# Eight stores of values in the second half: issued from ScalarE's queue in place of GpSimd's

## The chip, the cores and the metric

The kernel runs on one core of one Trainium2 chip. The metric is the device time of one execution in microseconds. The core has five instruction queues: TensorE (PE, with its weight loads PEld), VectorE (DVE), ScalarE (ACT), GpSimd (POOL) and SyncE (SP). DMAs are issued from the queues of SP, ACT and GpSimd and all run on the core's 16 DMA engines.

## The reference

One layer of a streaming encoder over two groups with the same weights: a prompt of 2048 tokens and a sample of 32, model width 1024. Cut to what matters:

```python
h = rmsnorm(x, g_pre_mix)
z = h @ w_in                                   # 1024 -> 512 + 4 * 512
u, zq, zf, zi, zg = split(z)                   # zi: the values of the recurrence
y_pool = pool_mix(u, ...)                      # trailing-window means, per-group map
q, f, k = silu(zq), lb + (1 - lb) * sigmoid(zf), (1 - lb) * sigmoid(-zf)
S1, o = hgrn_run(S0, q, k, zi, log(f))         # 4 heads x 128, state 128 x 128 per head
y_hg = rmsnorm(o, g_hg_norm) * silu(zg)
x = x + rmsnorm(concat(y_pool, y_hg) @ w_out, g_post_mix)
f = (silu(h2 @ w_gate) * (h2 @ w_up)) @ w_down # h2 = rmsnorm(x, g_pre_ffn), 1024 -> 2816 -> 1024
x = x + rmsnorm(f, g_post_ffn)
```

Everything is in float32.

## The kernel before

The prompt is worked through in two halves of 1024 tokens, the sample beside the second. Each half has the stages values and projections with recurrence (`front`), output projection (`project`), and `gate_up`; `down` comes once behind both. A float32 product is made of three matmuls of a high and a low part (`fhi`, `flo` for activations, `wf` for weights). In the second half the projections are made by a seven-product scheme: `front_pairs` runs over eight pairs of column blocks, each with seven products of twelve 128x512 matmuls, and accumulates them in PSUM banks that the code calls `gx`, `gz`, `gy`. For the first pair (f and q of head 0) the products stand in the order gx, gz, gx, gy, gx, gy, gx. The weight forms of each product lie in DRAM (`wd`) and are loaded as two tiles `wf` three products ahead (`fetch`, L929).

Ahead of them `values` multiplies the 1024 tokens by the 512 value columns. It fills all eight PSUM banks (`vps`), four of the pool MM and four of AX. In its last round it copies each bank to a tile `vt` of 128 x 4 x 128, four on ScalarE and four on VectorE in turn (L809), and stores each in DRAM (`vd`, four heads of 128 x 8 x 128, in pieces of 512 bytes) from GpSimd's queue (L810). Later `hgrn` loads the values of one head as `vh` (L1192). The same PSUM banks are then taken by gx, gz and gy.

What follows on the other engines for the first pair, with the lines that the prediction names:

- ScalarE copies the first gx to c (L956); PE then goes on in the same bank with the third product. VectorE adds gz to c (L959). ScalarE makes two sigmoids sg of c (`use`, L864 and L868), the first with a load of its function table ahead of it, then copies gx to another c (L967) and gy to a third (L971); the fifth product adds to the bank that L967 reads.
- In between, ScalarE and VectorE finish the high and low parts `hhi` and `hlo` of the first half's hidden values (L1525, L1528), SP stores them (`hdFalse`, L1530), and SP loads `xwv` (L817), weights for the sample's values (`vsps`).

`vt`, `c`, `sg`, `wf`, `xwv`, `hhi`, `hlo` and some others share the buffers of one pool, `tp`, with one tag and 25 buffers of 128 x 512 float32. A tile gets a buffer that an earlier tile has done with, and its first writer waits until the last reader of that one has ended; for vt the last reader is its store.

PE's order is the order of the program: small tasks are mixed in between products at points that a count of PE's planned time (`Pace.t`, `poll`) gives. The order of the other queues is chosen by the framework when the program is built, from the program's order and a plan of its own.

Of the kernel before, what the change touches and what calls it, by code (L numbers as in the profile page):

```python
# [84 lines left out]
def body(tc, ins, outs, cst):  # L85
    nc = tc.nc
    ctx = ExitStack()
    with ctx:
# [15 lines left out]
        def mmbank(name="mmb"):  # L104
            return MM.tile([P, 512], F32, tag="mm", name=name)

        def axbank(name="axb"):
            return AX.tile([P, 512], F32, tag="ax", name=name)
# [4 lines left out]
        def t2(name, shape=None, dt=F32):  # L113
            return TP.tile(shape or [P, 512], dt, tag="t", name=name)
# [90 lines left out]
        def mm(out, l, r, start, stop, ns, more=False):  # L205
            nc.tensor.matmul(out, l, r, start=start, stop=stop, skip_group_check=more)  # L206
            Pace.t += ns

        def rcost(n):
            return max(107.0, n / 2.4 + 2.5)  # L210
# [19 lines left out]
        def poll():  # L230
            for tk in list(Pace.tasks):
                if tk.done or (tk.after is not None and not tk.after.done):
                    continue
                if tk.ready <= Pace.t:
                    tk.step()
# [57 lines left out]
        def take(look=LOOK):  # L293
            i = Stream.used
            Stream.used += 1
            ahead(i + 1 + look)
            r = Stream.items[i]
            Stream.items[i] = None
            return r

        def in_turn(trios):

            for a, b in ((0, 2), (0, 3), (1, 2)) if len(trios) > 1 else ((0, 2), (1, 2), (0, 3)):
                for t in trios:
                    yield t[a], t[b]
# [134 lines left out]
        vd = DP.tile([NH, P, NCH, P], F32, name="vd")  # L440
# [351 lines left out]
        def values(S, pairs):  # L792
            pss = [mmbank("vps") for _ in range(4)] + [axbank("vps") for _ in range(4)]
            for k in range(0, KD, 2):
                _, hi, lo = take(1)
                while S.seen[0] < k + 2:
                    S.norm.step()
                if k == 4:
                    next(pairs)
                for i in range(8):  # L800
                    c0 = i % 4 * P
                    trios = [(*(x[:, kk * 512 + c0:kk * 512 + c0 + P] for x in S.plain[i // 4][k // 2]), hi[kk], lo[kk]) for kk in range(2)]
                    for n, (a, b) in enumerate(in_turn(trios)):
                        mm(pss[i], a, b, k == 0 and n == 0, k + 2 == KD and n == 5, rcost(512))
                        if n % 3 == 2:
                            poll()
                    if k + 2 == KD:
                        vt = t2("vt", [P, NH, P])
                        (nc.vector.tensor_copy if i % 2 else nc.scalar.copy)(vt, pss[i].rearrange("p (h c) -> p h c", c=P))  # L809
                        nc.gpsimd.dma_start(out=vd[:, :, i, :].rearrange("h p c -> p h c"), in_=vt)  # L810
            Smp.mix = Task(sample_mix(), 4000.0)

        def sample_values():
# [1232 lines left out]
        with tc.manual_schedule(engines={mybir.EngineType.PE}):  # L2046
            for i, S in enumerate(halves):
                if i:
                    while S.seen[0] < 1:
                        S.norm.step()  # L2050
                    pairs = front_pairs(S)
                    values(S, pairs)
                if i == 0:
                    halves[1].st = CP.tile([P, 64], F32, name="st_b")
                    Task(later_stats(halves[1]), 25000.0)
                    Task(mixed_weights(), 4000.0)
                if i:
                    next(pairs, None)
                else:
                    for h in range(NH):  # L2060
                        head_products(S, h)
                    for g in (3, 2, 1, 0):
                        pool_products(S, g)
                S.gpm = row_vector("g_post_mix")
                for tg in range(2):
                    project(S, tg)
                if i == 0:
                    forms = Task(weight_forms(), 50000.0)
                gate_up(S, second_start if i == 0 else (lambda: down_first(halves)))
            last = down(halves)  # L2070
            for tk in list(Pace.tasks):
                tk.finish()
# [42 lines left out]
```

## Time and profile before

| | |
|---|---|
| median of three runs | 2081.92 us (2081.21 to 2084.04) |
| profiled execution, its time | 2080.79 us |
| profiled execution, its span | 2079.0 us |
| mean granted clock of TensorE | 0.995 |
| DMA over the span | 389.15 MB, 187 GB/s |
| the stage of the change | 840 to 911 us of the span |

A time in the profile is in microseconds from the start of the span. A row of a timeline has start, busy time, engine, line, operation, output<-input, shape, and in brackets how long the engine sat idle before it and what released it. A row of the waits says who waited for whom: total, times, longest. "issue" is time in which an engine waited for nothing that the profile shows. A queue's DMA issue is listed by the time that the queue spent on it; "landing" is from the issue to the arrival of the last byte.

### The profile page before, as it was taken

The numbers are of one execution on the slowest core, as the hardware profiler recorded it, in microseconds if no ns is written. First come the engines' busy times: TensorE is split into PE (matmuls) and PEld (weight loads), VectorE is DVE, ScalarE is ACT, GpSimd is POOL, SyncE is SP. The second block draws the span as 40 slices with busy tenths as digits, with TensorE's granted clock in tenths as the row PEclk, the third lists the DMA queues.
The fourth block names the chain that finished last, engine by engine and source line by source line (L and its number), as shares of the span: only waits on it lengthen the run. The fifth ranks groups of instructions, "written<-read, shape, count | busy, mean of one in ns | idle before, by whom it ended". The sixth has DMA issues, their size and how long they took to land.

```text
span 2079.0 us, 34579 instructions
## 1 busy us (share of the span) xinstructions
PE 2050.9 (99%) x12980; PEld 1669.0 (80%) x12980; DVE 1464.9 (70%) x2252; ACT 850.8 (41%) x1689; POOL 413.9 (20%) x484
## 2 busy tenths in 40 slices
PE   9999999999999999799999999999999999999998
PEld 8788888888888887678887788888888778888876
DVE  5555674799887888666676697776666766566587
ACT  6544344654554544333344563444444521011032
POOL 0223421212222221333242100000000210110134
PEclk9999999999999999899999999999999999999999
DMA  8633344537787778464573614554445797776779
GB/s 290 200 101 113 103 142 143 171 109 236 226 245 216 219 217 253 152 239 151 194 267 132 193 51 137 163 149 145 138 142 167 235 336 221 220 224 200 220 199 225
DMA packets 427672, 389.15 MB, mean 187 GB/s; under 512 B 22360, under 2 KB 324432, under 8 KB 427504
## 3 DMA queue, kind: packets, MB, share of 16 engines
q1 hardware_dynamic: 424288, 376.65, 57.7%
q0 software_dynamic: 2784, 9.70, 2.2%
q8 instruction: 103, 1.69, 0.3%
q14 instruction: 65, 0.53, 0.1%
q10 hardware_dynamic: 432, 0.57, 0.1%
HBM read 251.77 MB, written 135.07 MB: 186 GB/s over the span
## 4 chain that ended last, share of the span: by engine, by line
PE 93%; DVE 4%; issue 1%; ACT 1%; DMA 1%; POOL 1%; DVEq 0%; SPq 0%; ACTq 0%; POOLq 0%
PE gx L206 26%; PE gy L206 13%; PE dx L206 11%; PE ops L206 9%; PE mmb L206 8%; PE gz L206 6%; PE dy L206 5%; PE vps L206 4%; PE dz L206 3%; PE gb L206 1%; PE gw L206 1%; PE gsps L206 1%; PE tps L349 1%; PE ups L206 1%; DVE acc L1887 1%
## 5 line engine op out<-in xcount | busy, mean ns | idle before, releaser
L206 PE MATMUL gx<-fhi,wf 128*128 128x512 f32 x1632 | 464.5, 393 | 13.0 <-ACT c L967 11.4
L206 PEld LDWEIGHTS gx<-fhi,wf 128*128 128x128 f32 x1632 | 304.5, 188 | 78.6 <-ACT c L967 11.8
L206 PE MATMUL gx<-flo,wf 128*128 128x512 f32 x816 | 256.1, 393 | 0.0
L206 PE MATMUL gy<-fhi,wf 128*128 128x512 f32 x832 | 239.9, 391 | 1.0 <-DVE c L1709 1.0
L206 PE MATMUL dx<-dhi,hst 128*128 128x512 f32 x640 | 185.4, 391 | 0.8 <-DVE acc L1887 0.7
L206 PEld LDWEIGHTS gy<-fhi,wf 128*128 128x128 f32 x832 | 155.4, 188 | 33.4 <-ACT wf L1598 1.6
L206 PEld LDWEIGHTS gx<-flo,wf 128*128 128x128 f32 x816 | 153.8, 188 | 32.3
L1603 DVE TENSOR_TENSOR wf<-s,wf 128x512 fp32r<-128x512 f32 x176 | 136.7, 783 | 58.6 <-ACT wf L1598 57.1
L1887 DVE TENSOR_TENSOR acc<-dx,acc 128x512 f32<-128x512 f32 x168 | 115.0, 689 | 71.1 <-PE dx L206 70.2
L206 PEld LDWEIGHTS dx<-dhi,hst 128*128 128x128 f32 x640 | 119.6, 188 | 29.9 <-issue 3.4
L1598 ACT CAST wf<-s 128x512 fp32r<-128x512 f32 x176 | 107.0, 620 | 73.5 <-PE gy L206 17.4
L206 PE MATMUL gy<-flo,wf 128*128 128x512 f32 x416 | 131.1, 392 | 0.0
L1826 ACT CAST dhi<-t 128x1024 fp32r<-128x1024 f32 x20 | 20.6, 1054 | 252.8 <-DVE dlo L1827 183.9
L1813 POOL TENSOR_TENSOR t<-wdr 128x1024 f32<-128x1024 f32 (+1 forms) x6 | 13.4, 2226 | 514.3 <-DMA wdr<-in_w_down_dram 506.2
L1598 ACT CAST wf<-wraw 128x512 fp32r<-128x512 f32 x132 | 80.6, 621 | 79.2 <-PE gx L206 35.9
L206 PE MATMUL gz<-fhi,wf 128*128 128x512 f32 x384 | 112.5, 393 | 0.0
L1603 DVE TENSOR_TENSOR wf<-wraw,wf 128x512 fp32r<-128x512 f32 x132 | 94.4, 722 | 24.5 <-ACT wf L1598 24.3
L206 PE MATMUL dx<-dlo,hst 128*128 128x512 f32 x320 | 98.7, 390 | 0.0
L206 PE MATMUL dy<-dhi,hst 128*128 128x512 f32 x320 | 98.6, 389 | 0.0
L206 PEld LDWEIGHTS gy<-flo,wf 128*128 128x128 f32 x416 | 78.1, 188 | 16.9 <-issue 0.8
L206 PE MATMUL mmb<-hTlo,whi 128*128 128x512 f32 x256 | 90.1, 409 | 0.0
L1887 DVE TENSOR_TENSOR acc<-dy,acc 128x512 f32<-128x512 f32 x88 | 60.6, 689 | 38.6 <-PE dy L206 38.0
(381 smaller groups left out, 4153.2 us busy)
## 6 DMA issues: line engine op xcount, KB each, us to landing
hst<-hdFalse SPq DMA_DIRECT2D x140, 256.0 KB, 2.9
hst<-hdTrue SPq DMA_DIRECT2D x140, 256.0 KB, 3.6
wf<-wd SPq DMA_DIRECT2D x112, 256.0 KB, 5.1
wraw<-in_w_gate_dram SPq DMA_DIRECT2D x50, 512.0 KB, 4.3
wraw<-in_w_up_dram SPq DMA_DIRECT2D x50, 512.0 KB, 4.5
hdFalse<-hhi SPq DMA_DIRECT2D x77, 256.0 KB, 4.0
hdFalse<-hlo SPq DMA_DIRECT2D x77, 256.0 KB, 2.7
hdTrue<-hhi SPq DMA_DIRECT2D x77, 256.0 KB, 2.3
```

The costliest lines, as they stand in the source:

```text
L206: nc.tensor.matmul(out, l, r, start=start, stop=stop, skip_group_check=more)
L349: nc.tensor.transpose(ps[:, c:c + P], xn[:, (2 * kp + kk) * P:(2 * kp + kk + 1) * P], ident)
L1598: nc.scalar.copy(wf[:, 0], getattr(M, src) if isinstance(src, str) else src)
L1603: nc.vector.tensor_tensor(wf[:, 1], getattr(M, src) if isinstance(src, str) else src, wf[:, 0].bitcast(F32), ALU.subtract)
L1813: nc.gpsimd.tensor_tensor(W.t1, b12, b11, ALU.subtract)
L1826: nc.scalar.copy(hi, src)
L1887: nc.vector.tensor_tensor(dst, ps, dst, ALU.add)
```

## The change

The eight stores of vt in `values` are issued from ScalarE's queue. The copies, the tiles, the target and the sizes stay.

```diff
                     if k + 2 == KD:
                         vt = t2("vt", [P, NH, P])
                         (nc.vector.tensor_copy if i % 2 else nc.scalar.copy)(vt, pss[i].rearrange("p (h c) -> p h c", c=P))
-                        nc.gpsimd.dma_start(out=vd[:, :, i, :].rearrange("h p c -> p h c"), in_=vt)
+                        nc.scalar.dma_start(out=vd[:, :, i, :].rearrange("h p c -> p h c"), in_=vt)
```

## The prediction

> **What bounds the kernel now.** I read the page first, for the share of each engine, and then the stage around the change. PE is busy nearly the whole span, so the time is that of PE's work plus the places where PE stands still.
>
> ```profile
> span 2079.0 us, 34579 instructions
> PE 2050.9 (99%) x12980; PEld 1669.0 (80%) x12980; DVE 1464.9 (70%) x2252; ACT 850.8 (41%) x1689; POOL 413.9 (20%) x484
> ```
>
> 2079.0 less 2050.9 leaves 28.1 us in which PE does nothing. The waits of the stage of the stores (each row: us in all, times, longest) show where the largest part lies; the last two rows are SP's queue, the first of them in this stage, the other later.
>
> ```profile
> POOL vd L810 <- issue: 16.3, 5, 4.7
> ACT L864 <- DMA vd<-vt: 14.4, 1, 14.4
> PE gx L206 <- ACT c L967: 11.4, 1, 11.4
> SPq L929 <- DMA vd<-vt: 12.6, 2, 9.0
> ...
> SPq L929 <- DMA wf<-wd: 4.5, 10, 1.3
> ```
>
> The wait of 11.4 us is one wait, 41% of all that PE loses. It begins at the changed line: PE waits for the copy of c (L967) on ACT; that copy stands behind the sigmoid sg (L864), which needs a buffer of the pool `tp`; the buffer still holds a vt whose store GpSimd has not brought out. SP's loads of wf wait for the same stores. The queues of ACT and GpSimd, in order of time (start us, busy us):
>
> ```profile
> 854.02 1.07 ACT L809 COPY vt<-vps 128x512 f32<-128x512 f32 x2
> 854.97 0.63 ACT L1525 CAST hhi<-hs 128x512 fp32r<-128x512 f32 x1
> 855.49 0.60 ACT L809 COPY vt<-vps 128x512 f32<-128x512 f32 x1
> 857.86 0.59 ACT L809 COPY vt<-vps 128x512 f32<-128x512 f32 x1 [1.77 <-PE vps L206]
> ...
> 861.98 0.59 ACT L956 COPY c<-gx 128x512 f32<-128x512 f32 x1 [3.02 <-DVE hs L1521]
> 877.00 1.28 ACT L864 ACT_TABLE_LOAD   x1 [14.42 <-DMA vd<-vt]
> 878.29 0.63 ACT L864 ACTIVATE sg<-c 128x512 f32<-128x512 f32 x1
> 879.80 0.63 ACT L868 ACTIVATE sg<-c 128x512 f32<-128x512 f32 x1 [0.88 <-DMA vd<-vt]
> ...
> 880.84 0.58 ACT L967 COPY c<-gx 128x512 f32<-128x512 f32 x1
> ```
> ```profile
> 854.93 1.02 POOL L810 DMA_DIRECT2D vd<-vt  x1 [2.33 <-ACT vt L809]
> ...
> 872.51 0.75 POOL L810 DMA_DIRECT2D vd<-vt  x1 [3.53 <-issue]
> 877.23 0.76 POOL L810 DMA_DIRECT2D vd<-vt  x1 [3.97 <-issue]
> ```
>
> The landing of these eight, from issue (the answer for the tile vt):
>
> ```profile
> DMA to landing us min/median/max: 2.5/3.2/5.1
> ```
>
> I number the stores 0 to 7. The data of all eight are in vt by 862.5 (the last copy, below), yet GpSimd sends store 4 at 872.5 and store 5 at 877.2. ACT goes on at 877.0, when store 4 has landed, and L868 at 879.8, when store 5 has. Between two stores GpSimd waits for nothing that the profile shows ("issue", 16.3 us in five waits): the pace is GpSimd's own. The transfers themselves are short, 2.5 to 5.1 us.
>
> The chain that ended last gives the price on PE (start us, us):
>
> ```profile
> 861.90 2.73 PE gz L206 x12
> ...
> 877.23 2.55 DMA vd<-vt
> ...
> 881.48 5.09 PE gx L206 x12
> 886.57 0.69 PE gy L206 x3
> 887.26 0.99 PE vsps L206 x8
> 888.25 2.28 PE gy L206 x9
> 890.53 5.44 PE gx L206 x24
> ```
>
> A product of twelve matmuls takes 2.72 (5.44 for two). From the end of gz (864.64) to the start of the gx at 890.53 are 25.89 us, in which PE does four products and eight small matmuls: 4 x 2.72 + 0.99 = 11.87. So 25.89 - 11.87 = **14.0 us** are lost: 11.4 of standing still, 2.4 in the product after it (5.09 against 2.72), 0.2 beside them. The slow product is the clock, seen in the stretches below (busy us of PE, PEld, DVE, ACT, POOL, then granted clock, DMA share, GB/s).
>
> ```profile
> 859.00:870.00 11.00, 11.00 (x49) 8.83 (x47) 4.80 (x8) 0.59 (x1) 2.29 (x3) 1.00 0.93 295
> 870.00:875.00 5.00, 0.06 (x1) 0.00 (x0) 0.00 (x0) 0.00 (x0) 0.75 (x1) 0.73 0.56 157
> 875.00:882.00 7.00, 0.52 (x1) 0.50 (x2) 1.75 (x3) 4.02 (x6) 1.51 (x2) 0.50 0.43 173
> 882.00:889.00 7.00, 7.00 (x27) 4.59 (x26) 1.39 (x2) 1.14 (x2) 0.76 (x1) 0.72 0.41 140
> 889.00:911.00 22.00, 22.00 (x279) 16.99 (x277) 16.49 (x39) 6.40 (x12) 6.57 (x12) 1.00 1.03 367
> 911.00:1059.00 148.00, 146.95 (x1940) 118.62 (x1929) 94.07 (x201) 52.88 (x150) 52.39 (x83) 1.00 0.49 166
> ```
>
> A mean of 0.73 over five us that begin with the wait, at 0.50 afterwards, is 2.3 us at full clock: a wait below about 2.3 us costs no clock here.
>
> **The change, part by part.** *Removed:* eight stores from GpSimd's queue, 0.75 to 1.02 us each, and the 16.3 us between them. GpSimd does not bound the stage (2.3 of 11 us busy), so its own time is worth nothing; what counts is that buffers 4 and 5 come free. That takes away up to 14.0 us of PE's path.
>
> *Added on ACT:* eight DMA issues, each behind its copy. Four of the copies are DVE's, so ACT now also waits for DVE. Prices: an issue as SP's for the same shape (256 KB in 512-byte pieces, the stores of hhi), a landing as above or as those of SP between 855 and 900 (second row); the last row is that tile over the whole kernel.
>
> ```profile
> L1530 SPq DMA_DIRECT2D hdFalse<-hhi x4: 371/404/467, 859.3 to 895.0; - x4
> ```
> ```profile
> DMA to landing us min/median/max: 2.2/5.1/5.4
> ```
> ```profile
> DMA to landing us min/median/max: 2.1/3.0/9.0
> ```
>
> DVE is late with its copies, because it makes flo until 858.1:
>
> ```profile
> 858.14 0.68 DVE L1528 TENSOR_TENSOR hlo<-c,hhi 128x512 fp32r<-128x512 f32 x1
> 858.74 1.88 DVE L809 COPY vt<-vps 128x512 f32<-128x512 f32 x3
> 860.54 0.68 DVE L1528 TENSOR_TENSOR hlo<-hs,hhi 128x512 fp32r<-128x512 f32 x1
> 861.25 0.69 DVE L1521 TENSOR_TENSOR hs<-c,hs 128x512 f32<-128x512 f32 x1
> 861.86 0.68 DVE L809 COPY vt<-vps 128x512 f32<-128x512 f32 x1
> 864.73 0.69 DVE L959 TENSOR_TENSOR c<-gz,c 128x512 f32<-128x512 f32 x1 [1.58 <-PE gz L206]
> ```
>
> I take the order of the program for ACT's queue. Store 0 goes at 854.7. Store 1 waits until DVE's first copy ends, 858.74 + 0.68 = 859.42; everything of ACT behind it waits too, 4.3 us, which costs PE nothing yet, since ACT had free time until 861.98. From 859.45 ACT has, ahead of the end of c (L956): seven issues at 0.40 = 2.8; copies of vt 2, 4, 6, of which 4 and 6 must end before their store goes, 0.53 + 0.59 + 0.59 = 1.7; two casts hhi behind which the queue moves on in 0.53 each = 1.1; c itself 0.6. Sum 6.2, so c ends at 865.6 and not at 862.6. DVE's hlo at 860.54 needs the first of these casts and moves by about 0.5, its last copy to 863.0, still ahead of store 7. PE writes on into the bank that c reads when gz ends, at 864.64: **1.0 us** late.
>
> The compiled program has eight completion counters for the DMAs of SP and ACT together, given out in turn, and a DMA waits until the one eight places earlier has landed (SP's wait for its own earlier wf, 4.5 us in ten times, is that). GpSimd's stores had counters of their own. Store 7 comes eight places behind store 2, issued until about 861.3; with a landing L it can go at 861.3 + L and not at 864.1: no loss for L up to 2.8, 2.6 us at 5.4. I take 0.6, near GpSimd's median of 3.2, since the same eight stores gave it. ACT's part is then **1.6 us** (1.0 to 3.6).
>
> *SP's queue:* its loads no longer wait for GpSimd, but now share the DMA engines with the stores in a shorter time. Up to the second wf of the product at 886.57 SP has 15 transfers, and ACT seven, from about 859.5: 22 x 0.262 MB = 5.8 MB, at the 367 GB/s of the busiest stretch 15.7 us, so until 875.2. PE asks for it at 864.64 + 1.6 + 3 x 2.72 = 874.4. **0.8 us** late. Lower end 0, as PE never stood still from 889 to 911 at share 1.03. Upper end 3: from 859 to 911 the stretches move 3.2 + 0.8 + 1.2 + 1.0 + 8.1 = 14.3 MB, which at 330 GB/s (between the 295 and the 367) takes 43.2 us, against the 52 - 14.0 + 2.4 = 40.4 that are left. Behind 911 the share is 0.49 and nothing is owed.
>
> *sg's buffer and c (L967):* PE's order is written by hand and stays. Store 4 goes at about 862.5 and lands by 865.7 to 867.9. After c, sg's table load and two sigmoids and hhi take 1.28 + 2 x 0.63 + 0.53 = 3.1 us; at 1.6 late they end about 870.3, and c (L967) at 870.9, just ahead of the end of gy at 864.64 + 1.6 + 5.44 = 871.7. Cover 0.8 us; where store 4 lands late that is the next thing to be late, and its cost lies in the upper ends above.
>
> **Sum:** -14.0 + 1.6 + 0.8 = -11.6 us. Against the profiled execution (2080.79, span 2079.0 and 1.8 around it) 2069.2; the median 2081.92 stands 1.1 higher, so **2070.3 us**.
>
> **The rivals.**
> *The whole 14.0 comes.* The planner that orders the queues may put the stores of the odd tiles behind ACT's other work, or the loads are in time. For it: PE did not stall once from 889 to 911. 2081.92 - 14.0 = 2067.9; chance 0.20 (2066.5 to 2068.5).
>
> *Loads of wf come late.* ACT's part is 3.6, the loads cost 3 and the clock 0.4: 14.0 - 7.0 = 7.0, so 2074.9; chance 0.16 (2073 to 2077.7). For it: DMA share 0.93 to 1.03 on both sides of the gap, which was where the queue caught up.
>
> *The counters bind ACT and SP together, and it gets slower.* Store 7 goes at 861.3 + L, so c ends 1.5 later and PE stands L - 1.8. Store 7 lands another L later; the third xwv load takes its counter ahead of the wf of the product at 886.57, which lands a third L later, at 862.4 + 3L, when PE asks at 871 + L: 2L - 9 late. With the 2.4 of the clock the loss is 3L - 8.4: it eats the 14.0 at L = 7.5 and gives slower by 0.2% (4.2 us) from L = 8.9; at 9.0, the longest landing of that shape, 2081.92 + 4.6 = 2086.5. Against it: 5.4 is the longest in this stage. Chance 0.09, of which 0.06 within 0.2% and 0.03 slower.
>
> *The change does not do what it says.* If the transfers and not GpSimd's issuing set the pace, ACT waits as long for the same buffers: 2081.9. Against it: landing 2.5 to 5.1 us, and a DMA share of 0.43 to 0.56 while PE stood still. Chance 0.05. The Trainium skill, page "DMA: Bandwidth & Descriptors", section "Issuing engines are not separate DMA queues", has a rule on this side: DMAs of all issuers run on the same 16 engines, and another issuer "will only save the time on the sequencer". By that rule alone the move would save GpSimd some 0.4 us a store and PE nothing. The trace differs on what that sequencer time is: 16.3 us in the waits between the stores.
>
> **How the numbers follow.** The sum's own case (2068.5 to 2073) has 0.50, the others 0.20, 0.16, 0.09, 0.05. 0.2% (4.2 us, about what a measurement of this kernel can tell from no change) is passed by the first three: faster 0.86; same 0.06 + 0.05 = 0.11; slower 0.03. The range from 2066.5 to 2076.5 leaves out the last two and the top of the late loads.
>
> **What would show it.** The eight issues on ACT's queue between 854 and 866, ACT waiting about 4 us for DVE's vt; no wait of ACT L864 or SP for vd; PE's wait for c (L967) gone, one of 1 to 2 us for c (L956) in its place; clock 1.00 from 870 to 890; DMA share near 1 from 860 to 897. The prediction is wrong if ACT stands at a store past 866, if PE waits for wf, or if PE's later waits (28.1 - 11.4 = 16.7 us in the whole kernel) grow.

## The result, and the profile after

The changed kernel takes 2070.93 us (median of six runs, 2068.38 to 2074.47); the kernel before took 2081.57 us beside it (2080.48 to 2084.04). That is 10.6 us less: ratio 0.9949, 95% interval 0.9936 to 0.9961, or 8.1 to 13.3 us. The forecast was 2070.3 us, 11.6 us less. The profiled execution took 2072.88 us.

The page of the changed kernel begins:

```profile
span 2070.9 us, 34565 instructions
PE 2051.7 (99%) x12980; PEld 1668.4 (81%) x12980; DVE 1466.9 (71%) x2252; ACT 850.4 (41%) x1689; POOL 406.8 (20%) x476
```

PE stands still for 2070.9 - 2051.7 = 19.2 us instead of 28.1. Of the waits in the stage (same columns as before, 850 to 890 us) the one of 11.4 us is gone. PE has two short ones in its place, and SP's loads no longer wait 12.6 us for vd:

```profile
ACT hhi L1525 <- issue: 1.8, 1, 1.8
...
PE gy L206 <- DMA wf<-wd: 1.3, 1, 1.3
...
PE gx L206 <- ACT c L956: 0.5, 1, 0.5
```

ACT's queue in order of time shows where they come from:

```profile
858.36 5.20 ACTq L810 DMA_DIRECT2D vd<-vt  x2
863.65 0.59 ACT L809 COPY vt<-vps 128x512 f32<-128x512 f32 x1 [5.32 <-PE vps L206]
864.14 0.62 ACT L1525 CAST hhi<-hs 128x512 fp32r<-128x512 f32 x1
864.27 0.93 ACTq L810 DMA_DIRECT2D vd<-vt  x2
865.24 0.59 ACT L809 COPY vt<-vps 128x512 f32<-128x512 f32 x1 [0.48 <-ACT hhi L1525]
865.86 1.07 ACTq L810 DMA_DIRECT2D vd<-vt  x2
866.97 0.59 ACT L809 COPY vt<-vps 128x512 f32<-128x512 f32 x1 [1.14 <-DVE vt L809]
867.59 1.73 ACTq L810 DMA_DIRECT2D vd<-vt  x2
869.36 0.62 ACT L1525 CAST hhi<-c 128x512 fp32r<-128x512 f32 x1 [1.80 <-issue]
869.88 0.58 ACT L956 COPY c<-gx 128x512 f32<-128x512 f32 x1
870.48 1.28 ACT L864 ACT_TABLE_LOAD   x1
```

The two stores of the first row with ACTq span 5.20 us: ACT issues store 0, then stands at store 1 until DVE has made its copy. The rest follows in 7 us (863.56 to 870.46), in the order of the program. sg (L864) no longer waits for a buffer. c (L956) ends at 870.46, half a microsecond after gz, and PE waits for it. The chain that ended last names the other wait (start us, us):

```profile
868.26 6.26 DMA vd<-vt
...
874.53 0.33 SPq L817
...
875.39 4.77 DMA wf<-wd
...
880.29 0.93 PE gy L206 x3
881.22 0.99 PE vsps L206 x8
882.22 2.28 PE gy L206 x9
884.50 5.44 PE gx L206 x24
```

The landing of the last store, a load of xwv on SP, a load of wf, and the sixth product behind them. Loss in the stage is read in all runs in the same way: from the first matmul of gz to the start of the seventh product (the row "PE gx x24"). Free of any wait that is 2.90 + 11.87 = 14.8 us by the sum; the three runs below in which PE waits nowhere measure 15.0. Before it was 861.74 to 890.53, 28.8 us, so 14.0 lost; now, with the first rows of gz and of the two waits,

```profile
867.09 0.61 PE L206 MATMUL gz<-fhi,wf 128*128 128x512 f32 x2
...
870.51 0.73 PE L206 MATMUL gx<-fhi,wf 128*128 128x512 f32 x2 [0.54 <-ACT c L956]
...
880.29 0.70 PE L206 MATMUL gy<-fhi,wf 128*128 128x512 f32 x2 [1.32 <-DMA wf<-wd]
```

it is 884.50 - 867.09 = 17.4 us, 2.6 lost. The clock stays at full speed, and the DMA engines are full once the queue has caught up (columns as in the prediction):

```profile
859.00:870.00 11.00, 10.97 (x49) 8.76 (x47) 7.33 (x10) 2.92 (x6) 0.00 (x0) 1.00 0.72 212
870.00:875.00 5.00, 4.49 (x20) 3.71 (x21) 2.30 (x4) 4.00 (x6) 0.00 (x0) 1.00 1.09 356
875.00:882.00 7.00, 5.68 (x29) 3.61 (x27) 2.08 (x3) 1.73 (x3) 0.00 (x0) 1.00 1.07 394
882.00:889.00 7.00, 7.00 (x34) 5.68 (x31) 3.10 (x6) 1.73 (x3) 1.50 (x3) 1.00 1.07 389
```

So in these two profiles the stage gained 11.4 us and the span 8.1. The stage began 5.3 us later (867.09 against 861.74), and what follows it took 2.1 us less: 11.38 - 5.35 + 2.07 = 8.1. The first of the experiments below looks at the 5.3 us.

### The profile page after: what moved, and what is told of

It reads as the page before. It is cut to its first block, busy times and chain, and to the rows that moved or that the text cites. A ratio compares the mean times of both kernels' runs of the same rounds, so it can differ in the third digit from the quotient of the medians.

```text
span 2070.9 us, 34565 instructions
## 1 busy us (share of the span) xinstructions
PE 2051.7 (99%) x12980; PEld 1668.4 (81%) x12980; DVE 1466.9 (71%) x2252; ACT 850.4 (41%) x1689; POOL 406.8 (20%) x476
## 4 chain that ended last, share of the span: by engine, by line
PE 66%; DVE 5%; issue 2%; DMA 1%; ACT 1%; POOL 1%; SPq 0%; ACTq 0%; DVEq 0%; POOLq 0%
PE gx L206 22%; PE gy L206 11%; PE dx L206 10%; PE gz L206 5%; PE dy L206 5%; PE ops L206 5%; PE dz L206 3%; PE gsps L206 1%; DVE acc L1887 1%; DMA wf<-wd 1%; PE gb L206 1%; PE sacc L206 1%; PE gw L206 1%; POOL xT L373 0%; DMA xT<-x_channels 0%
```

## The experiments

All stages are measured as above. "Lost" is the stage less 14.8, of which 0.2 is no wait. Where a recorded expectation counts from the end of gz, its figures are 2.9 us smaller than these. Times are medians, in brackets that of the kernel before, run beside it; "one" marks a single run. Kernels with the same bracket ran in one series.

| run | first gz, seventh product | stage | lost | time us |
|---|---|---|---|---|
| before | 861.74, 890.53 | 28.8 | 14.0 | 2081.57 |
| before again | 864.33, 893.15 | 28.8 | 14.0 | 2081.87, one |
| changed | 867.09, 884.50 | 17.4 | 2.6 | 2070.93 (2081.57) |
| changed again | 862.06, 881.23 | 19.2 | 4.4 | 2070.71 (2082.01) |
| changed, third time | 864.20, 883.41 | 19.2 | 4.4 | 2072.46 (2082.34) |
| odd stores on SP | 863.18, 879.21 | 16.0 | 1.2 | 2069.35 (2082.01) |
| GpSimd, own buffers | 866.46, 881.45 | 15.0 | 0.2 | 2070.58 (2082.01) |
| GpSimd, 2 KB rows | 863.02, 881.48 | 18.5 | 3.7 | 2070.81 (2082.01) |
| stores 4, 5 on ACT | 863.88, 883.92 | 20.0 | 5.2 | 2075.51, one (2080.35) |
| GpSimd, own buffers, 2 KB rows | 863.38, 878.37 | 15.0 | 0.2 | 2067.95 (2080.35) |
| the same again | 860.92, 875.91 | 15.0 | 0.2 | 2066.86 (2082.34) |
| ACT, 2 KB rows | 861.28, 880.89 | 19.6 | 4.8 | 2069.73, one (2080.35) |
| ACT, own buffers | 863.43, 879.25 | 15.8 | 1.0 | 2068.48 (2082.34) |

The theory was the prediction's: sg waits for buffers that GpSimd's slow issuing keeps, and ACT's issuing is fast. The rivals: the transfers set the pace, whoever issues; or what counts is something else that ACT's queue moves.

**How steady the stage and the time are.** The two kernels as they are, each profiled again, the changed one also timed in two further series.

> The changed kernel once more, to see what of its 8 us in the profile belongs to the stage and what to the execution. From the end of gz to the start of the seventh product (gx) before had 25.89 us and after 14.53. If the gain is the stage's, this comes out again within 0.5 us (14.0 to 15.0), with the same two waits: PE for c (L956) 0.5 us and for wf 1.3 us, both within 1 us of that. The stage's start was 5.3 us later in the after profile; the theory that this is the execution and not the change (PE's wait for c of L1709 near 505 us, 2.5 in place of 1.0, lies 350 us ahead of the first moved instruction) says that it differs here again. A rival, that the change shifts earlier work through another order, says it comes out again at 5.3. Time 2070.9, ratio 0.993 to 0.996.

> The kernel before once more, one look. What belongs to the kernel comes out again: from the start of the second product (gz) to the start of the seventh (gx) 28.6 us, with PE's wait of about 11.4 us for c (L967). What belongs to the execution may differ: PE's wait for c of L1709 near 504 us (1.0 in before, 2.5 in after), and PE's wait of 1.0 us near 970 us, which none of the later profiles has. If that last wait is the kernel's (SP still behind with its loads), it is here again at 0.8 to 1.2 us; if it is the execution's, it is gone. Time 2080.5 to 2084.

> The changed kernel, unaltered, beside e9 on the same chip. Theory: gz to the seventh product 17 to 19.5 us, with a wait for c (L956) of 0.5 to 2.1 and one for wf of 1.3 to 2.2; 2070 to 2072 us. Rival (these waits are chance of two executions): 15 to 16 us and 2068 to 2069.

The stage of before repeats to 0.1 us (28.8 and 28.8). That of after was expected to repeat within 0.5 and does so only within 2 (17.4, 19.2, 19.2). The difference is c (L956). In the two executions of 19.2 us PE waited 2.09 and 2.10 us for it, in the first 0.54. The row of the third execution for the second wait names ACT:

```profile
869.18 0.73 PE L206 MATMUL gx<-fhi,wf 128*128 128x512 f32 x2 [2.10 <-ACT c L956]
...
879.20 0.70 PE L206 MATMUL gy<-fhi,wf 128*128 128x512 f32 x2 [1.55 <-ACT sg L864]
```

No gy reads sg. In the first execution the same matmul began at 880.29 while that sigmoid ran from 879.79 to 880.42, so it is not what PE waits for; the wait is the same one for wf, put down to what ended beside it.

The start of the stage moves from one execution to another, in the changed kernel alone by 5.0 us (862.06 to 867.09), so the rival that the change itself brings 5.3 us is out. One source is a wait far ahead of it, near 505 us, which was 1.0 us before and 2.5 after; the kernel before, profiled again, has it too (2.45 us). Another is the clock: near 820 us PE waits 2.0 to 2.25 us in all thirteen profiles, and in five of them, the first of the changed kernel among them, slow matmuls follow (last section). Both belong to the execution and not to the change. So does the wait of 1.0 us near 970 us: the kernel before, again, does not have it. A total therefore settles 2 us badly; the stage, read together with its waits, settles less than 1. Over three series the totals gained 10.6, 11.3 and 9.9 us, and the stages 11.4, 9.6 and 9.6.

**Is it ACT's queue in particular?** The odd stores, those of DVE's copies, on SP's queue; the even ones on ACT's.

```diff
-nc.gpsimd.dma_start(out=vd[:, :, i, :]..., in_=vt)
+(nc.sync if i % 2 else nc.scalar).dma_start(out=vd[:, :, i, :]..., in_=vt)
```

> ScalarE sends only the stores of its own four copies, SP those of VectorE's. Theory that ScalarE's waiting for VectorE and its eight issues made the remaining loss (c of L956 0.5 us late, store 7 late, then the wf): ScalarE ends c (L956) ahead of the end of gz, store 7 goes earlier, the wf comes earlier; of the 2.7 us that the stage still loses 1.5 to 2 come back, time 2069. Rival, that the eight common completion counters and the shared DMA engines make it: the same number of transfers with common counters stands in front of the same wf, now in SP's own queue; the loss stays 2 to 4 us, time 2071 to 2072.

ACT no longer stands at DVE's copies, and c is on time; its row ends at 863.97, ahead of gz's end, and one wait of PE is left in the stage. ACT's timeline, then PE's:

```profile
863.38 0.59 ACT L956 COPY c<-gx 128x512 f32<-128x512 f32 x1 [1.28 <-PE gx L206]
```
```profile
875.00 0.70 PE L206 MATMUL gy<-fhi,wf 128*128 128x512 f32 x2 [0.78 <-DMA wf<-wd]
```

Stage 16.0: the term for ACT's queue is real and is removed in this way, and the loads of wf stay late by 0.8. In time, 1.4 us below the changed kernel of the same series, which the ranges (2068.42 to 2071.65 against 2069.41 to 2072.48) do not separate.

**Is it the buffer?** GpSimd issues as before, but vt lies two to a buffer in another pool, so that no sigmoid can wait for a store.

```diff
-vt = t2("vt", [P, NH, P])
+vp = vp if i % 2 else ztile("vp", [P, 2, NH, P]); vt = vp[:, i % 2]
```

> Stores on GpSimd as in the kernel before, but the vt tiles lie in the pool of the large buffers (two to a buffer of 4 KB), not in the pool that sg, wf and xwv share. Theory of the buffers (PE waited only because sg and wf needed the buffers that unsent stores held): GpSimd's pace stays (store 0 to store 7 over some 28 us, some 16 us of waits between them), yet the wait of ScalarE for vd and PE's 11.4 us are gone; the stage takes 12 to 14 us, time 2067 to 2070. Rival, that GpSimd's busy time or its descriptor writing slows the stage: nothing changes, 2081.5. The planner orders VectorE's copies earlier in this one, which alone can give at most about 1 us.

GpSimd is no faster than before (first four and last of its eight stores, then the landing of all eight):

```profile
855.62 1.02 POOL L810 DMA_DIRECT2D vd<-vp  x1
859.72 0.78 POOL L810 DMA_DIRECT2D vd<-vp  x1 [3.08 <-DVE vp L809]
864.99 0.75 POOL L810 DMA_DIRECT2D vd<-vp  x1 [4.49 <-issue]
867.84 0.76 POOL L810 DMA_DIRECT2D vd<-vp  x1 [2.10 <-issue]
...
891.90 0.76 POOL L810 DMA_DIRECT2D vd<-vp  x1 [5.04 <-DVE tt L1034]
```
```profile
DMA to landing us min/median/max: 2.5/5.0/6.6
```

It ends its last store at 892.7, 37 us behind the start of the first, and yet PE waits nowhere in the stage (15.0 us). So the 14.0 us came through the buffers: in this stage the slow issuing itself costs nothing. (The profile puts some of the gaps down to work such as tt, which a store of vt does not need; it names only what ended last.) The time does not show the better stage: 2070.58 us, just above the expected range, against 2070.71 for the changed kernel in the same series. In the two profiles the stage began 4.4 us later here (866.46 against 862.06).

The first rival, that the transfers set the pace whoever issues, is answered by the changed kernel: the same eight transfers from ACT's queue leave no wait of ACT L864 for vd. What that rival had right is in the next run.

**What makes GpSimd slow?** The same bytes from GpSimd in four times longer rows: the target is laid out by tile, so that a store is 128 pieces of 2 KB instead of 512 of 512 bytes. The later load of vh reads the 512-byte pieces.

```diff
-vd = DP.tile([NH, P, NCH, P], F32, name="vd")
+vd = DP.tile([NCH, P, NH * P], F32, name="vd")
-nc.gpsimd.dma_start(out=vd[:, :, i, :]..., in_=vt)
+nc.gpsimd.dma_start(out=vd[i], in_=vt.rearrange("p h c -> p (h c)"))
-nc.sync.dma_start(out=vh, in_=vd[h])
+nc.sync.dma_start(out=vh, in_=vd[:, :, h * P:(h + 1) * P].rearrange("n p c -> p n c"))
```

> Stores on GpSimd and buffers as in the kernel before; only the layout of vd in DRAM changes, so that a store has 128 pieces of 2 KB in place of 512 of 512 bytes (the four later loads of vh get the 512-byte pieces). Theory that GpSimd's pace is set by the number of pieces that its descriptors hold at once: the waits between the stores fall from 16.3 us to under 4, the last store goes at about 866 and not 882.9, PE's 11.4 us go, the stage takes 12 to 14 us, time 2067 to 2070. Rival, a fixed time of GpSimd per store (about 4 us whatever the shape): the last store stays at 880 or later, time 2080 to 2082. Second rival, that 512-byte pieces move slowly: landing falls well below the 3.2 us, issues keep their distance.

GpSimd's timeline, and the eight by the tile vt:

```profile
856.26 0.81 POOL L810 DMA_DIRECT2D vd<-vt  x1 [2.34 <-ACT vt L809]
861.06 3.77 POOL L810 DMA_DIRECT2D vd<-vt  x7 [4.00 <-DVE vt L809]
```
```profile
L810 POOL DMA_DIRECT2D vd<-vt x8: 539/540/808, 856.3 to 864.3; - x8
```

Seven stores back to back, 3.77 / 7 = 0.54 us each, where before there were 3 to 5 us from one to the next. So neither the bytes nor a fixed time for each store sets the pace. The pieces do, by their number or their length, which change together here.

What GpSimd waits for with 512 pieces can be read from the trace of before, store by store (us):

| store | issued | landing | landed at | next store issued |
|---|---|---|---|---|
| 1 | 859.85 | 2.7 | 862.55 | 862.82 |
| 2 | 862.82 | 5.1 | 867.92 | 868.23 |
| 3 | 868.23 | 4.0 | 872.23 | 872.51 |
| 4 | 872.51 | 4.4 | 876.91 | 877.23 |
| 5 | 877.23 | 2.5 | 879.73 | 880.08 |
| 6 | 880.08 | 2.5 | 882.58 | 882.91 |

Each store goes about 0.3 us after the one before it has landed. It is the same in the kernel before, profiled again, and with own buffers, where the landings of stores 3 to 6 are 5.0 to 6.6 us and the gaps grow with them. With 2 KB rows it is not so: store 1, issued at 861.06, lands at 863.8, when four more have gone out. Nor is it so on ACT's queue: in the changed kernel store 2 goes at 864.27, while store 1, issued at 863.2 with a landing of 2.3, is under way. So on GpSimd's queue the transfers do set the pace of stores of 512 pieces, as the first rival said; on ACT's they do not. What in GpSimd holds the next store back is not shown.

The time is that of the changed kernel without any move to ACT (2070.81 against 2070.71 in the same series). ACT L864 still waits 3.0 us for vd (14.4 before), which costs PE nothing. The stage is 18.5, above the expected range, for a new reason: PE waits for wf three times, 0.71, 0.30 and 1.65 us.

**The whole move, or two stores?** Only stores 4 and 5, which held the two buffers, on ACT's queue.

```diff
+(nc.scalar if i in (4, 5) else nc.gpsimd).dma_start(out=vd[:, :, i, :]..., in_=vt)
```

> Only stores 4 and 5, those whose buffers the two sigmoids need, go from ScalarE's queue; 0 to 3, 6 and 7 stay on GpSimd. Theory that unsent stores hold PE in two places, by sg on ScalarE and right behind it by the loads of wf on SP (which need the buffers of stores 6 and 7): ScalarE waits no more, but store 6 goes at about 872 and store 7 at 877, so the wf of the sixth product lands at 880 to 882 and PE waits there 6 to 9 us and loses some clock; from gz to the seventh product 22 to 26 us (28.6 before, 17.2 and 19.0 after), time 2074 to 2079. Rival, that sg alone held PE: 15 to 17 us, time 2068 to 2071.

c and sg are on time, but 5.2 us are lost, most of them in the sixth product. SP's waits for vd (us in all, times, longest), and then PE:

```profile
SPq L929 <- DMA vd<-vt: 6.4, 2, 3.4
SPq L817 <- DMA vd<-vt: 5.8, 2, 3.7
```
```profile
878.08 1.19 PE L206 MATMUL gy<-fhi,wf 128*128 128x512 f32 x2 [3.16 <-DMA wf<-wd]
```

SP's loads need buffers which GpSimd's remaining stores still keep. The theory holds in kind and not in size: the stage of 20.0 lies below its 22 to 26 and above the rival's 15 to 17. The expected 6 to 9 us of waiting were 3.2, and slow matmuls followed: the first two took 1.19 us instead of 0.7. So the move of all eight does two things: it frees sg's buffers and those of SP's loads.

**Do pieces matter on ACT's queue?** The changed kernel with the 2 KB rows.

> The changed kernel with vd in rows of 2 KB: eight stores on ScalarE's queue, each 128 pieces in place of 512. Theory that ScalarE's late c (L956) comes of the number of its issues, its waits for VectorE and store 7's counter, and the late wf of bytes in a burst: pieces matter little, an issue takes 0.3 to 0.35 in place of 0.43 us, c is late by 0.5 to 2 us, wf by 0.5 to 2; from gz to the seventh product 16 to 19 us. Rival, that the 512-byte pieces are what is slow to move: both waits fall below 0.5, 14.6 to 15.5 us. Time 2068 to 2071.

No: 19.6 us in one execution, far from the rival and a little above the theory's own range, with waits of 1.41 for c and 2.16 for wf. An issue fell from 0.43 to 0.36 us (median).

**What the remaining 2.6 to 4.4 us are.** Own buffers and 2 KB rows on GpSimd; then own buffers with ACT issuing.

> Stores on GpSimd, vt in the pool of the large buffers as in the third run, and vd in rows of 2 KB as in the fourth, so GpSimd sends them fast. Nobody waits for a vt's buffer, ScalarE issues nothing, and the stores' counters are GpSimd's own. Theory that what the changed kernel still loses on wf is the burst (eight stores at once on the shared DMA engines make the hhi store and the wf land late): the wait for wf returns, 0.7 to 2.5 us in all; from gz to the seventh product 15.3 to 17 us. Rival, that it is the common counters or ScalarE's queue alone: no wait for wf, 14.6 to 15.0 us as in the third run. Time by both 2067.5 to 2071, too close to tell.

> GpSimd issues the stores again, in 2 KB rows, and vt has buffers of its own (two to a buffer): the kernel of e7, timed against the changed kernel on the same chip. Theory (GpSimd's pace went by the pieces of a store, and with own buffers DVE's copies come earlier, so that stores and loads of wf are spread): gz to the seventh product 15.0 us, no wait of PE in it, 2067 to 2069 us, 1.5 to 3 us below the changed kernel. Rival (e7 was an execution with short waits elsewhere): 2070 to 2072, as the changed kernel.

> The changed kernel with buffers of vt's own (as in e3), so that ACT still issues all eight stores but DVE's copies are ordered earlier. Theory A (what is left is ACT's queue: c (L956) stands behind the issues and the stores share completion counters with SP's loads): c late by 0.5 to 2 and wf by 1 to 2 all the same, gz to the seventh product 17 to 19 us. Theory B (what is left comes from DVE's late copies, which hold ACT's queue and crowd the stores into 8 us): no wait or below 0.8 in sum, 15.0 to 15.8 us. Time 2068 to 2072 either way.

With own buffers the planner puts DVE's first copies earlier: they begin 6.2 us ahead of the first gz with ACT issuing, and 3.0 to 4.6 us ahead of it in the three executions of the changed kernel. On GpSimd the stage has no wait left, twice; the wait for wf that I expected to return did not. On ACT it is 15.8, as theory B has it: c still 0.53 late, wf on time, though the queue and its completion counters are those of the changed kernel. By the profile SP even stood 3.1 us at a load of wf for one of the stores, which here share no buffer with it. So the counters alone do not make wf late. What differs is when the stores' bytes flow (stretches of 852 to 860, 860 to 868 and 868 to 884 us; changed kernel, then ACT with own buffers, then the first stretch of GpSimd with own buffers and 2 KB rows, second run of it):

```profile
852.00:860.00 8.00, 8.00 (x37) 6.63 (x36) 7.97 (x5) 5.33 (x6) 4.33 (x2) 1.00 0.10 29
860.00:868.00 8.00, 8.00 (x38) 6.60 (x36) 6.33 (x9) 2.28 (x4) 0.00 (x0) 1.00 0.62 187
868.00:884.00 16.00, 14.14 (x64) 10.18 (x63) 4.38 (x7) 6.37 (x10) 0.00 (x0) 1.00 1.08 366
```
```profile
852.00:860.00 8.00, 8.00 (x37) 6.63 (x36) 6.51 (x8) 3.21 (x7) 2.31 (x1) 1.00 0.61 183
...
868.00:884.00 16.00, 16.00 (x75) 12.31 (x74) 6.43 (x11) 5.79 (x11) 1.51 (x3) 1.00 1.05 356
```
```profile
852.00:860.00 8.00, 8.00 (x37) 6.61 (x36) 7.96 (x11) 5.16 (x7) 3.52 (x7) 1.00 0.79 253
```

From 868 on the engines are full in all three (share 1.05 and more), so whatever was not moved by then shares them with the loads of wf. The engines were nearly idle from 852 to 860 in the changed kernel: 29 GB/s times 8 us are 0.23 MB, less than one store of 0.262 MB. With own buffers on ACT it is 183 x 8 = 1.5 MB, with those and long rows on GpSimd 253 x 8 = 2.0 MB. The other variants but one stand in this order, though the stretch is fixed and the first gz lies between 860.9 and 867.1: those with 0.2 to 0.5 MB in that stretch (changed, three times; GpSimd with 2 KB rows; ACT with 2 KB rows) waited 1.3 to 2.7 us for wf, the one with 0.9 (odd stores on SP) 0.8, those with 1.1 to 2.0 none. The exception is the kernel with two stores on ACT, whose loads waited for buffers. One megabyte at the 366 GB/s of the stretch behind is 2.7 us. So the late wf goes together with late bytes. That the bytes are its cause is argued and not shown: in the same kernel SP's queue is late as well. In the changed kernel's first profile it stands 3.7 us at two stores of hhi, which ACT casts between and behind its own issues, and 1.3 us at loads of xwv for stores of vd (the chain above); the loads of wf come behind both. No run here takes one of the three away and leaves the others.

The version with own buffers and 2 KB rows on GpSimd is the fastest: 2066.86 us (2065.58 to 2070.86) against 2072.46 (2069.49 to 2073.45) for the changed kernel in the same series, and 0.9932 of before (0.9918 to 0.9946). The medians stand 5.6 us apart, the ranges overlap, and the stage explains 4.2 of it (15.0 against 19.2).

## Why the prediction was right

- *The loss of 14.0 us and its cause.* Right. Of all steps this one decides. Own buffers alone, with GpSimd as slow as ever, gave the stage 15.0 us, the one that the arithmetic of the products gives (14.8). The wait of PE for c (L967) and the slow clock in the stage are gone together in both kernels: clock 1.00 from 870 to 889.
- *GpSimd's pace is its own.* Only half right. The prediction held the short landings (2.5 to 5.1 us) against the rival that the transfers set the pace. Read one by one, those landings are the pace: each store of 512 pieces on GpSimd's queue goes 0.3 us after the one before has landed. Right is that the move does away with this, since ACT sends a store while the last is under way. The forecast needed only that. Of the two arguments against the rival's 2081.9 one holds, the DMA share of 0.43 to 0.56 while PE stood still; the short landings do not speak against it. So here a right conclusion came from an incomplete reading, which is luck in part.
- *The eight issues on ACT.* Place and order right, with ACT's wait for DVE's first copy (forecast about 4 us; 5.20 for two stores with it). c (L956) was forecast 1.0 us late and another 0.6 for the counter, 1.6; PE waited 0.54, 2.09 and 2.10. The 0.6 has the wrong reason: in the first profile store 2, whose counter store 7 takes, had landed at 866.5 (864.27 and 2.2), and store 7 goes at 868.26, right behind store 6. The term that was short is the seven issues, 0.40 each or 2.8 in all: they took 3.8 and 3.7 us in the first two profiles, the last of them 1.06 and 1.00. That gives 1.0 + 1.0 = 2.0 us late, as in the two executions of 2.1. In the first one DVE's copies began 4.6 us ahead of gz in place of 3.0, which hid most of it. Why the last issues are longer the profile does not say. Odd stores on SP take the whole term away.
- *The loads of wf.* Forecast 0.8 late, measured 1.32, 1.55 and 1.55. In the execution whose stage began nearest to that of before (862.06) PE asked at 875.5 in place of 874.4, as c was later, and the product began at 877.0. The term that was mis-sized is the rate, 367 GB/s from 859.5 until 875.2. That execution moved 295 GB/s from 859 to 870 and 382 from 870 to 875, 5.2 MB together; at 406 GB/s behind 875 the 5.8 MB are reached at about 876.6. The sum of bytes fits in this way, which does not show that nothing else held the loads (above).
- *Cover of sg and c (L967).* Right, and larger than said: 1.9 us in all three profiles of the changed kernel in place of 0.8. No run with all eight stores on ACT waited there.
- *The clock.* The prediction put a wait below about 2.3 us at no cost. In the stage this held for waits of up to 2.16 us, but by luck: elsewhere waits of 2.12 to 2.23 us cost clock (last section).
- *The signs of being wrong.* One that the prediction named did come: PE waits for wf. It contradicts the prediction's own sum, which has 0.8 us of that wait. ACT's last issue ended at 869.3 in the first profile of the changed kernel, past the 866 named, but in a stage 5.3 us later; in the second it ended at 865.8. PE's later waits did not grow beyond what executions differ by: 17.3 us in the first profile of the changed kernel and 15.6 in the second, besides the waits for c (L956) and wf, against 16.7.
- *The sum.* 2.4 us given back, measured 2.6 to 4.4 (the waits, and 0.8 of slower first matmuls behind them and small gaps), so 9.6 to 11.4 gained in the stage against 11.6. That the time came within 0.6 us (2070.93 against 2070.3) is closer than the terms were; single executions of the changed kernel differ by more.
- *Behind 911 nothing owed*: the stage's gain was not given back later. From the seventh product to the end the three profiles of the changed kernel take 1186.2 to 1187.2 us, the two of before 1187.0 and 1188.5. What made the profiled span 8.1 and not 11.4 us shorter lies ahead of the stage.
- *The rivals.* The whole 14.0 did not come in this kernel, but own buffers bring it. Late wf was right in kind, and at 1.3 to 1.6 less than the 3 that this rival took. The counters' chain stands in the trace link for link (store 7, xwv, wf), with a landing of 6.26 us; by its formula 3 x 6.26 - 8.4 = 10.4 would have been lost. It was 2.6: the formula took that landing for every store, but the trace has the landing of three of them, and the other two are 2.2 and 2.3.

```profile
DMA to landing us min/median/max: 2.2/2.3/6.3
```

- *The issuer is indifferent.* By the rule of the Trainium skill ("DMA: Bandwidth & Descriptors", section "Issuing engines are not separate DMA queues") the move should have been worth a sequencer's issue time, "usually small relative to the DMA itself". The runs agree that the engines are shared in so far as wf came late with GpSimd as issuer too (2 KB rows). They differ on the small: on GpSimd's queue a store of 512 pieces took the landing of the one before it, and held buffers turned that into 14.0 us of PE's path.

## What to carry to other kernels

A slow queue costs where a buffer waits for it: look at what the stores hold, not at how busy the issuer is. Here three edits took the same wait away (another issuer, fewer and longer pieces, buffers of its own), and by the stage the best of them left the issuer alone. An issuer that waits for nothing in the profile may be waiting for its own last transfer: set each landing beside the next issue. When the wait is gone, the bytes that it held back meet the next loads; ask how early a store can go, since here the kernels that moved more ahead of the full stretch waited less.

## What was not expected of the hardware

- GpSimd's pace: a store of 512 pieces goes 0.3 us after the one before has landed, which left 16.3 us of waiting between eight stores. With 128 pieces and the same bytes there is no waiting between seven (0.54 us each, landings of 2.7 to 7.1 us). On ACT's queue stores of 512 pieces overlap, and the longer rows only move an issue from 0.43 to 0.36 us.
- The clock: near 505 us waits for c (L1709) of 2.32, 2.35 and 2.36 us (GpSimd with 2 KB rows, with own buffers, ACT with own buffers) were followed by matmuls at the usual pace, 0.70 for the first two and 0.63 for the next. Waits of 2.45 (the kernel before, again) and 2.51 (the changed kernel) were followed by matmuls at a lower clock, 1.05 for the next two. That looks like a limit between the two, but near 820 us waits for c (L1727) of 2.12 to 2.23 us were followed by a lower clock in five executions (changed; odd stores on SP; GpSimd with own buffers; the same with 2 KB rows, in one of its two runs; two stores on ACT), and waits of 1.99 to 2.25 us by the usual pace in the other eight. So a wait of about 2.2 us costs clock in one execution and not in another; its length alone does not decide it. Rows of GpSimd with own buffers, then of the first run that also has the 2 KB rows:

```profile
508.17 0.70 PE L206 MATMUL gy<-fhi,wf 128*128 128x512 f32 x2 [2.35 <-DVE c L1709]
508.71 0.63 PE L206 MATMUL gy<-flo,wf 128*128 128x512 f32 x2
```
```profile
819.45 0.73 PE L206 MATMUL vps<-whw,fhi 128*128 128x512 f32 x2 [2.12 <-DVE c L1727]
820.02 0.86 PE L206 MATMUL vps<-wlw,fhi 128*128 128x512 f32 x2
820.68 1.05 PE L206 MATMUL vps<-whw,flo 128*128 128x512 f32 x2
```
